# A tile's scale moved from VectorE to TensorE, and the first tile in two parts, at the start of an encoder layer

## The chip, the cores and the metric

The kernel runs on one core of a Trainium2 chip. The metric is the device time of one execution in microseconds (us), as the median of several runs. A profiled execution gives a trace of every instruction of the core's engines: TensorE (PE for matmuls, PEld for the weight loads ahead of them), VectorE (DVE), ScalarE (ACT), GpSimd (POOL), SyncE (SP, which issues DMAs), and of the transfers.

## What is computed

One layer of an encoder on x of 1024 tokens by 1024 channels, all in float32. What matters here is its beginning:

```
mod = silu(c) @ w_ada + b_ada                  # six vectors of 1024: sh1, sc1, gt1, sh2, sc2, gt2
h   = rmsnorm(x, norm1_g) * (1 + sc1) + sh1
z   = h @ w_in                                 # u, v, q, k, va and two gates
```

After that come a gated MLP branch and a windowed attention branch on z, a merge, an output projection, and a SwiGLU feed-forward layer that is modulated in the same way by the other vectors. The output has the shape of x.

## The kernel before, in words

Channels lie on the 128 partitions and tokens along the free axis, so x is eight tiles of 128 channels (k = 0 to 7) by 512 tokens for the first half of the tokens. Products keep float32 accuracy by splitting each operand into a high part (rounded, type fp32r) and a low part (the remainder) and by adding three products: high·high, high·low and low·high.

The part at issue is the first part of `half(0)`, from line 570 on. There `in_order[0]` is true, so each engine issues its instructions in the order of the program text; SP's loads are in program order everywhere. Further on some stretches are in program order and some are ordered by the compiler's scheduler.

Before the tile loop (lines 579 to 654):

- SP issues the loads of x (`xt`, eight tiles), of c (`crow`), of the column constants `cc` (b_ada, two gains, gm_b_s), of r (the rows of w_ada for tile 0's scale and shift, two loads of 512 KB), then, at lines 591 to 595, the first half of `wq0` (256 KB), the scale half of `r1` (rows for tile 1's scale, 512 KB), the first half of `wk0`, the shift half of `r1`, and the second half of `wq0`. More `r` loads and weight units follow inside the loop (`r4`, in the text below, is the first pair that comes as one load of 1024 KB: the rows for tile 4).
- The squares of x are made on ScalarE (`square`) or VectorE (`square_dve`), added in pairs on VectorE, and summed over channels by TensorE (`column_sums`). ScalarE takes the root, VectorE the reciprocal (`rcol`), and four float32 matmuls spread it over the partitions into the PSUM bank `rp`.
- c is spread over the partitions by TensorE, and ScalarE makes `silu_c` from it (128 x 1024, every partition alike).
- A channel's scale or shift is a dot of one row of w_ada (transposed) with silu(c). `ada_dot` (line 211) does 128 of them at once on VectorE: one product of 128 x 1024 elements with an accumulated sum, into a column of `acc_mod`; a small ScalarE activation then adds bias and gain into a column of `mod`.
- Where TensorE would wait, `open_bank` and `keep_going` add products with zeros into banks that are used later: 7 of them (`ZEROS[2]`) at line 652 behind the four matmuls of `rp`.

In the tile loop (line 665 on), for each k: VectorE scales x by `mod` and by the root's reciprocal (`rp` for k = 0, its copy `rb` in SBUF after), ScalarE adds the shift and rounds to the high part `hH`, VectorE makes low parts of weights and runs `ada_dot` for the scale of tile k + 1, makes the low part `hL` of h, and runs `ada_dot` for the shift of tile k + 1. ScalarE casts weights to high parts between these. TensorE runs the passes of q and k products of tile k: high·high first, which needs `hH` and the high weights. At k = 2 it also sums the squares of the halo (128 tokens of the other half), at k = 4 and 7 it does the halo's products.

All helpers' instructions have line L79 in the profile (L131 for loads), so tiles tell them apart. In the profile's names: `mid<-mid,silu_c` is `ada_dot`; `mid<-mid,mod,at` and `mid<-mid,mod,ss` scale x; ScalarE's `h<-mid,mod` is `hH`, VectorE's `h<-mid,mod,h` is `hL`; `at<-identr,zeros` are the zeros, `at<-ident,rcol` the matmuls of `rp`; `mm<-wh,h` and `mm<-wl,h` are q products.

Of the kernel before, what the change touches and what calls it, by code (L numbers as in the profile page):

```python
# [8 lines left out]
F32 = mybir.dt.float32  # L9
F32R = mybir.dt.float32r  # L10
BF16 = mybir.dt.bfloat16
AF = mybir.ActivationFunctionType
ALU = mybir.AluOpType
# [3 lines left out]
P = 128  # L17
D = 1024
S = 1024
KT = D // P  # L20
HALF = 512
# [15 lines left out]
ZEROS = (9, 2, 7)  # L37
# [4 lines left out]
def kernel(  # L42
# [43 lines left out]
    V, A, G, T = (Engine(e) for e in (nc.vector, nc.scalar, nc.gpsimd, nc.tensor))  # L86
# [3 lines left out]
    const = ctx.enter_context(pool("const"))  # L90
# [17 lines left out]
    def at_bank():  # L108
        return psum.tile([P, 512], F32, tag="at", name=nm("at"))
# [7 lines left out]
    def midt(dt, shape):  # L117
        return mid.tile([P, 2048], dt, tag="mid", name=nm("mid")).rearrange(
            "p (a b) -> p a b", a=shape
        )  # L120
# [9 lines left out]
    def load(dst, src):  # L130
        tc.keep_in_program_order(nc.sync.dma_start(dst, src))  # L131
# [47 lines left out]
    epsc = const.tile([P, 1], F32, tag="epsc", name="epsc")  # L179
    V.memset(epsc, EPS)  # L180

    cc = const.tile([P, 72], F32, tag="cc", name="cc")
    bada, g1c, g2c, bsT = cc[:, :48], cc[:, 48:56], cc[:, 56:64], cc[:, 64:72]
    base = const.tile([P, 48], F32, tag="base", name="base")

    def load_cond():
# [9 lines left out]
    def silu_cond(pcs, i0=0):  # L196
        for i, pc in enumerate(pcs, i0):
            A.activation(silu_c[:, i * 512 : (i + 1) * 512], pc, AF.Silu)
# [9 lines left out]
                                   in1=g, op0=ALU.add, op1=ALU.mult)  # L208
        V.tensor_scalar(base[:, GT1:SH2], bada[:, GT1:SH2], 0.5, None, op0=ALU.mult)

    def ada_dot(r, col, cast=None, then=None):

        c1 = slice(col, col + 1)
        V.scalar_tensor_tensor(
            out=r, in0=r, scalar=1.0, in1=silu_c, op0=ALU.mult, op1=ALU.mult,
            accum_out=acc_mod[:, c1],
        )
        if then is not None:
            then()
        if cast is not None:  # L220
            A.copy(*cast)
        factor, added = 1.0, bada
        if GT1 <= col < SH2:
            factor, added = 0.5, base
        for sc, g in ((SC1, g1c), (SC2, g2c)):
            if sc <= col < sc + 8:
                factor, added = g[:, col - sc : col - sc + 1], base
        A.activation(mod[:, c1], acc_mod[:, c1], AF.Identity, bias=added[:, c1], scale=factor)

    def ada_pair(k):  # L230
        r = midt(F32, 2)
# [59 lines left out]
    def keep_going(bank, one, zero, n):  # L291

        for _ in range(n):
            T.matmul(bank, zero, one.unsqueeze(1).to_broadcast([P, 4, P]), start=False, stop=False)
# [272 lines left out]
    def half(hf):  # L567
# [4 lines left out]
        if hf == 0:  # L572
            in_order[0] = True
            xt2 = [midt(F32, 4) for _ in range(2)]
            xt = [xt2[k // 4][:, k % 4, :] for k in range(KT)]
            halo = midt(F32, 16)
            xh, qh = halo[:, :KT, :], halo[:, KT:, :]
            hl4 = midt(F32R, 16)

            for k, n in ((0, 2), (2, 2), (4, 2), (6, 1), (7, 1)):  # L580
                load(xt2[k // 4][:, k % 4 : k % 4 + n, :].rearrange("p a b -> p (a b)"),
                     xA[:, k * HALF : (k + n) * HALF])
                if k == 2:
                    load_cond()
            hd_store = lambda q, f: f(
                hd[0, q * HALF : (q + 1) * HALF, :].rearrange("(a p) t -> p a t", p=P), xt2[q])
            load(cc, cols)
            r = ada_pair(0)
            wq0, wk0 = (wpool.tile([P, UNIT], F32, tag="raw", name=nm("raw")) for _ in range(2))
            r1 = midt(F32, 2)  # L590
            load(wq0[:, :512], w_q[0][:, :512])
            load(r1[:, 0, :], w_ada1[1, :, :D])
            load(wk0[:, :512], w_kv[0][:, :512])
            load(r1[:, 1, :], w_ada1[1, :, D:])
            load(wq0[:, 512:], w_q[0][:, 512:])
            base_bias = bias_base()
            A.activation(sm(QPK, "es"), ones[:, :QPK], AF.Silu)
            build_bias(*base_bias, range(BIAS))

            total = at_bank()  # L600
            open_bank(total, zeros, zeros)
            keep_going(total, zeros, zeros, ZEROS[0])
            cond = silu_rows()
            sqs = [midt(F32, 4) for _ in range(2)]
            sq = [sqs[k // 4][:, k % 4, :] for k in range(KT)]
            add = lambda i, j: V.tensor_tensor(sq[i], sq[i], sq[j], op=ALU.add)
            square = lambda k: A.activation(sq[k], xt[k], AF.Square)

            def square_dve(k):
                V.tensor_tensor(sq[k], xt[k], xt[k], op=ALU.mult)  # L610

            def column_sums(q, last=False):

                for i in range(NT):
                    T.matmul(total[:, i * P : (i + 1) * P], q[:, i * P : (i + 1) * P], ones,
                             start=False, stop=last and i == NT - 1)

            square(0)
            square(1)
            add(0, 1)  # L620
            column_sums(sq[0])
            square(2)
            square_dve(3)
            add(2, 3)
            column_sums(sq[2])
            square_dve(5)
            square(4)
            silu_cond(cond[:1])
            add(4, 5)
            column_sums(sq[4])  # L630
            square(6)
            square(7)
            silu_cond(cond[1:], 1)
            add(6, 7)
            column_sums(sq[6], True)
            root = sm(5, "ms")
            A.activation(root[:, :NT], total.rearrange("p (a b) -> p a b", b=P)[:, :, 0], AF.Sqrt, scale=1.0 / D, bias=epsc)
            wq, wk = ([wpool.tile([P, UNIT], F32R, tag=x, name=nm(x)) for x in ("wh", "wl")]
                      for _ in range(2))
            ada_dot(r[:, 0, :], SC1, then=ada_base)  # L640
            V.reciprocal(rcol[0][:, :NT], root[:, :NT])
            A.copy(wq[0][:, :512], wq0[:, :512])
            ada_dot(r[:, 1, :], SH1)
            rp = at_bank()
            kbk = [at_bank() for _ in range(2)]
            open_bank(kbk[0], identr, zeros)
            keep_going(kbk[0], identr, zeros, ZEROS[1])
            for i in range(NT):
                T.matmul(rp[:, i * P : (i + 1) * P], rcol[0][:, i : i + 1].to_broadcast([P, P]), ident,
                         start=True, stop=True)  # L650
            open_bank(kbk[1], identr, zeros)
            keep_going(kbk[1], identr, zeros, ZEROS[2])
            hH = [hid(), hid()]
            hL = [hid(), hid()]
        else:
            hH, hL = h_next
            in_order[0] = True
# [7 lines left out]
        for k in range(KT):  # L665
            if hf == 0:
                x = xt[k]
                sh = mod[:, SH1 + k : SH1 + k + 1]
                if k < KT - 1:
                    r = ada_pair(k + 1) if k else r1  # L670
                V.scalar_tensor_tensor(
                    out=x, in0=x, scalar=mod[:, SC1 + k : SC1 + k + 1],
                    in1=rb if k else rp, op0=ALU.mult, op1=ALU.mult)
                A.activation(hH[k // 4][:, k % 4, :], x, AF.Identity, bias=sh)
                def low_part(w, w0, cs):
                    V.tensor_tensor(w[1][:, cs], w0[:, cs], w[0][:, cs].bitcast(F32), op=ALU.subtract)

# [13 lines left out]
                if k == 0:  # L691
                    rb = ss_tile()[:, :HALF]
                    A.copy(rb, rp)
                    tot4 = at_bank()
                    kbk.append(at_bank())
                    kps = [kbk[t // 2][:, (t % 2) * 256 : (t % 2 + 1) * 256] for t in range(nkv)]
                elif k == 2:
                    A.activation(qh, xh, AF.Square)
                elif k == 3:
                    A.activation(root[:, NT:], tot4[:, 0:1], AF.Sqrt, scale=1.0 / D, bias=epsc)  # L700
# [31 lines left out]
                    load(xh.rearrange("p a b -> p (a b)"), xA[:, KT * HALF :])  # L732
                cast = (w_next[0], raw) if src is not None else None
                if k < KT - 1:
                    ada_dot(r[:, 0, :], SC1 + k + 1, cast)
                if k == 3:
                    V.reciprocal(rcol[0][:, NT:], root[:, NT:])
                V.scalar_tensor_tensor(out=hL[k // 4][:, k % 4, :], in0=x, scalar=sh,
# [1185 lines left out]
def _layout(inputs):  # L1924
# [10 lines left out]
    def col(v):  # L1935
        return v.reshape(-1, 128).T

    a = {k: np.asarray(v) for k, v in inputs.items()}
    x = a["x"][0]
# [2 lines left out]
    w_b = a["w_b"][0].reshape(2, 4, 64, 1024).transpose(1, 0, 2, 3).reshape(512, 1024)  # L1942
    w_f = a["w_ffn_in"][0]
    ada = a["w_ada"][0].T.reshape(6, 8, 128, 1024)
    out = {
        "xA": np.concatenate([xt[:, t].reshape(8, 128, -1).transpose(1, 0, 2).reshape(128, -1)
                              for t in (slice(0, 512), slice(512, 640))], axis=1),
        "xB": xt[:, 512:],
        "c": a["c"][0],
        "cols": np.concatenate([col(a["b_ada"][0]), col(a["norm1_g"][0]), col(a["norm2_g"][0]),  # L1950
                                a["gm_b_s"][0].T], axis=1),
        "rowv": np.concatenate([a["gm_v_g"][0], a["q_norm_g"][0], a["k_norm_g"][0],
                                a["attn_sink"][0]]),
        "w_ada1": ada[[1, 0]].transpose(1, 2, 0, 3).reshape(8, 128, 2048),
        "w_ada2": ada[2:].reshape(32, 128, 1024),
        "w_u": tm(w_in[:, 0:512], 2),
        "w_v": tm(w_in[:, 512:1024], 2),
# [32 lines left out]
```

## Time and profile before

| | |
|---|---|
| median of 3 runs | 1226.87 us (1226.71 to 1227.76) |
| profiled execution | 1226.14 us, span in the trace 1224.2 us |
| VectorE busy | 898.1 us (73%) |
| ScalarE busy | 578.9 us (47%) |
| granted TensorE clock | 1.00 of full speed |
| DMA in the first 40 us | 15.03 MB at a mean of 376 GB/s |

The times are device times; the span is that of the instructions in the trace, 1.94 us shorter than the execution's time. All positions in the trace are us from the start of the span. Matmuls are pipelined and the ends of their records are modelled, so TensorE's waits are read from its weight loads.

### The profile page before, as it was taken

The numbers are of one execution on the slowest core, as the hardware profiler recorded it, in microseconds if no ns is written. First come the engines' busy times: TensorE is split into PE (matmuls) and PEld (weight loads), VectorE is DVE, ScalarE is ACT, GpSimd is POOL, SyncE is SP. The second block draws the span as 40 slices with busy tenths as digits, with TensorE's granted clock in tenths as the row PEclk, the third lists the DMA queues.
The fourth block names the chain that finished last, engine by engine and source line by source line (L and its number), as shares of the span: only waits on it lengthen the run. The fifth ranks groups of instructions, "written<-read, shape, count | busy, mean of one in ns | idle before, by whom it ended". The sixth has DMA issues, their size and how long they took to land.

```text
span 1224.2 us, 15615 instructions
## 1 busy us (share of the span) xinstructions
PE 1218.0 (99%) x5693; PEld 1015.8 (83%) x5693; DVE 898.1 (73%) x1450; ACT 578.9 (47%) x944; POOL 148.7 (12%) x178
## 2 busy tenths in 40 slices
PE   9999999999999999999999999999999999999998
PEld 7888888888888888888888888888888888888887
DVE  8988877788878766878797766675676766765646
ACT  5667855367855443635453233333333334433341
POOL 0024323114331000001000001010000000010001
PEclk9999999999999999999999999999999999999999
DMA  9721169621076333597413446445555439995542
GB/s 364 283 87 52 35 235 357 233 86 52 36 273 225 120 105 121 195 317 277 149 52 120 172 155 224 167 174 209 189 189 189 168 150 364 393 368 190 189 172 103
DMA packets 75936, 230.77 MB, mean 189 GB/s; under 512 B 8658, under 2 KB 8914, under 8 KB 71124
## 3 DMA queue, kind: packets, MB, share of 16 engines
q1 hardware_dynamic: 61444, 161.62, 37.4%
q0 software_dynamic: 14416, 68.17, 14.9%
q8 instruction: 44, 0.72, 0.2%
q14 instruction: 32, 0.26, 0.1%
HBM read 174.70 MB, written 55.05 MB: 188 GB/s over the span
## 4 chain that ended last, share of the span: by engine, by line
PE 98%; DMA 0%; DVE 0%; ACT 0%; issue 0%; SPq 0%; DVEq 0%; ACTq 0%
PE mm L79 51%; PE at L79 47%; DMA mid<-in_xA_dram 0%; DVE mid L79 0%; ACT mid L79 0%; ACT wh L79 0%; ACT h L79 0%; DVE crow L79 0%; ACT mod L79 0%; DVE zeros L79 0%; DVE ones L79 0%; SPq L131 0%; DVE identr L79 0%; DVEq L79 0%; ACTq L79 0%
## 5 line engine op out<-in xcount | busy, mean ns | idle before, releaser
L79 PE MATMUL mm<-mid,wh 128*128 128x512 f32 x704 | 217.4, 390 | 0.0
L79 ACT CAST wh<-raw 128x1024 fp32r<-128x1024 f32 (+1 forms) x151 | 154.4, 1024 | 118.7 <-PE mm L79 44.3
L79 DVE TENSOR_TENSOR wl<-raw,wh 128x1024 fp32r<-128x1024 f32 (+1 forms) x137 | 161.5, 1183 | 64.4 <-ACT wh L79 63.9
L79 PEld LDWEIGHTS mm<-mid,wh 128*128 128x128 f32 x704 | 131.7, 188 | 27.1
L79 PE MATMUL mm<-mid,wl 128*128 128x512 f32 x352 | 137.0, 389 | 0.0
L79 PE MATMUL mm<-wh,h 128*128 128x512 f32 x384 | 125.0, 397 | 0.2 <-ACT h L79 0.2
L79 PE MATMUL mm<-h,wh 128*128 128x512 f32 x400 | 123.9, 391 | 0.0
L79 PEld LDWEIGHTS mm<-h,wh 128*128 128x128 f32 x400 | 74.6, 188 | 15.3
L79 PE MATMUL at<-h,wh 128*128 128x512 f32 x272 | 84.0, 390 | 0.0
L79 PEld LDWEIGHTS mm<-wh,h 128*128 128x128 f32 x384 | 70.7, 188 | 14.6 <-ACT h L79 1.2
L79 DVE TENSOR_TENSOR wl<-ws,wh 128x1024 fp32r<-128x1024 f32 (+1 forms) x54 | 60.8, 1125 | 24.7 <-ACT wh L79 24.7
L79 PE MATMUL mm<-h,wl 128*128 128x512 f32 x200 | 77.9, 389 | 0.0
L79 PEld LDWEIGHTS mm<-mid,wl 128*128 128x128 f32 x352 | 66.1, 188 | 13.9
L79 ACT CAST wh<-ws 128x1024 fp32r<-128x1024 f32 (+1 forms) x54 | 52.5, 972 | 43.5 <-DVE ws L79 28.0
L79 PE MATMUL mm<-wl,h 128*128 128x512 f32 x192 | 71.2, 391 | 0.0
L79 ACT ACTIVATE t<-t 128x512 f32<-128x512 f32 x53 | 32.8, 630 | 72.8 <-DVE t L79 72.7
L79 PEld LDWEIGHTS at<-h,wh 128*128 128x128 f32 x272 | 50.9, 188 | 10.5
L79 DVE TENSOR_TENSOR ol<-raw,oh 128x1024 fp32r<-128x1024 f32 x30 | 36.6, 1224 | 30.0 <-ACT oh L79 30.0
L79 ACT ACTIVATE xs<-xs 128x512 f32<-128x512 f32 x21 | 13.3, 632 | 93.5 <-DVE xs L79 93.5
L79 PE MATMUL at<-h,wl 128*128 128x512 f32 x136 | 52.9, 389 | 0.0
L79 PE MATMUL at<-wl,wh 128*128 128x512 f32 (+1 forms) x136 | 52.7, 388 | 0.0
L79 PE MATMUL at<-wh 128*128 128x512 f32 (+1 forms) x136 | 52.7, 387 | 0.0
(271 smaller groups left out, 2731.1 us busy)
## 6 DMA issues: line engine op xcount, KB each, us to landing
raw<-in_w_gate_dram SPq DMA_DIRECT2D x28, 512.0 KB, 3.8
tA<-hid POOLq DMA_DIRECT2D x11, 1024.0 KB, 4.5
tB<-hid POOLq DMA_DIRECT2D x11, 1024.0 KB, 5.0
wo<-in_w_out_dram POOLq DMA_DIRECT2D x22, 512.0 KB, 5.8
wS<-wo POOLq DMA_DIRECT2D x11, 1024.0 KB, 5.1
raw<-wS SPq DMA_DIRECT2D x44, 256.0 KB, 3.3
raw<-tB SPq DMA_DIRECT2D x44, 256.0 KB, 4.5
mid<-in_w_ada_dram SPq DMA_DIRECT2D x20, 512.0 KB, 9.1
```

Of the source, the lines that this page charges most:

```text
L79: ins = f(*args, **kw)
```

## The change

The dot for tile 1's scale leaves VectorE. TensorE does it with eight float32 matmuls, into columns 256 to 383 of the bank `tot4`, whose allocation moves up. They stand where the 7 zero matmuls stood. The stationary operands are 128 x 128 blocks of r1's scale half, whose layout in memory is transposed by blocks for this on the host; the moving operand is one column of `silu_col`, repeated 128 times. `silu_col` is silu of c as 8 columns, and c comes as 8 more columns of `cc` (80 instead of 72). ScalarE's activation for tile 1's scale reads the dot from PSUM.

The load of r1's scale half now goes ahead of the first half of wq0. The square of x's tile 7 goes from ScalarE to VectorE. For k = 0, scaling x and making `hH` are each done in two parts of 256 columns, in turns.

```diff
-    cc = const.tile([P, 72], F32, tag="cc", name="cc")
+    cc = const.tile([P, 80], F32, tag="cc", name="cc")
+    ccol = cc[:, 72:80]
...
-    def ada_dot(r, col, cast=None, then=None):
+    def ada_dot(r, col, cast=None, then=None, dot=None):
         c1 = slice(col, col + 1)
-        V.scalar_tensor_tensor(
-            out=r, in0=r, scalar=1.0, in1=silu_c, op0=ALU.mult, op1=ALU.mult,
-            accum_out=acc_mod[:, c1],
-        )
+        if dot is None:
+            dot = acc_mod[:, c1]
+            V.scalar_tensor_tensor(out=r, in0=r, scalar=1.0, in1=silu_c, op0=ALU.mult, op1=ALU.mult,
+                                   accum_out=dot)
...
-        A.activation(mod[:, c1], acc_mod[:, c1], AF.Identity, bias=added[:, c1], scale=factor)
+        A.activation(mod[:, c1], dot, AF.Identity, bias=added[:, c1], scale=factor)
...
+            load(r1[:, 0, :], w_ada1[1, :, :D])
             load(wq0[:, :512], w_q[0][:, :512])
-            load(r1[:, 0, :], w_ada1[1, :, :D])
             load(wk0[:, :512], w_kv[0][:, :512])
...
             square(6)
-            square(7)
+            square_dve(7)
             silu_cond(cond[1:], 1)
+            silu_col = sm(KT, "silu_col")
+            A.activation(silu_col, ccol, AF.Silu)
...
             open_bank(kbk[1], identr, zeros)
-            keep_going(kbk[1], identr, zeros, ZEROS[2])
+            tot4 = at_bank()
+            dot1 = tot4[:, 2 * P : 3 * P]
+            for i in range(KT):
+                T.matmul(dot1, r1[:, 0, i * P : (i + 1) * P], silu_col[:, i : i + 1].to_broadcast([P, P]),
+                         start=i == 0, stop=i == KT - 1)
...
-                V.scalar_tensor_tensor(
-                    out=x, in0=x, scalar=mod[:, SC1 + k : SC1 + k + 1],
-                    in1=rb if k else rp, op0=ALU.mult, op1=ALU.mult)
-                A.activation(hH[k // 4][:, k % 4, :], x, AF.Identity, bias=sh)
+                for cs in (slice(0, HALF),) if k else (slice(0, 256), slice(256, HALF)):
+                    V.scalar_tensor_tensor(
+                        out=x[:, cs], in0=x[:, cs], scalar=mod[:, SC1 + k : SC1 + k + 1],
+                        in1=(rb if k else rp)[:, cs], op0=ALU.mult, op1=ALU.mult)
+                    A.activation(hH[k // 4][:, k % 4, cs], x[:, cs], AF.Identity, bias=sh)
...
-                    tot4 = at_bank()
...
-                    ada_dot(r[:, 0, :], SC1 + k + 1, cast)
+                    ada_dot(r[:, 0, :], SC1 + k + 1, cast, dot=None if k else dot1[:, :1])
...
+    ada1 = ada[[1, 0]].transpose(1, 2, 0, 3).reshape(8, 128, 2048)
+    ada1[1, :, :1024] = ada[1, 1].reshape(128, 8, 128).transpose(2, 1, 0).reshape(128, 1024)
```

More of the change, by code (lines that the diff above doesn't have):

```diff
@@ L1950, in _layout @@
         "cols": np.concatenate([col(a["b_ada"][0]), col(a["norm1_g"][0]), col(a["norm2_g"][0]),
-                                a["gm_b_s"][0].T], axis=1),
+                                a["gm_b_s"][0].T, col(a["c"][0])], axis=1),
         "rowv": np.concatenate([a["gm_v_g"][0], a["q_norm_g"][0], a["k_norm_g"][0],
                                 a["attn_sink"][0]]),
-        "w_ada1": ada[[1, 0]].transpose(1, 2, 0, 3).reshape(8, 128, 2048),
+        "w_ada1": ada1,
         "w_ada2": ada[2:].reshape(32, 128, 1024),
```

## The prediction

> **What bounds the kernel now.** I read the page first, then the waits of TensorE's weight loads in the first 40 us, then the timeline there engine by engine, then the DMA issues one at a time. The page and, below it, the waits (total, number of times, longest):
>
> ```profile
> span 1224.2 us, 15615 instructions
> PE 1218.0 (99%) x5693; PEld 1015.8 (83%) x5693; DVE 898.1 (73%) x1450; ACT 578.9 (47%) x944; POOL 148.7 (12%) x178
> PE 98%; DMA 0%; DVE 0%; ACT 0%; issue 0%; SPq 0%; DVEq 0%; ACTq 0%
> ```
> ```profile
> PEld mm L79 <- ACT h L79: 1.2, 3, 0.5
> PEld at L79 <- DVE rcol L79: 0.3, 1, 0.3
> PEld at L79 <- ACT mid L79: 0.2, 1, 0.2
> ```
>
> TensorE is busy for 1218.0 of 1224.2 us and 98% of the chain that ended last is its own work. The diff touches only what is issued before about 20 us and takes no matmul of the real work away. So it can win only TensorE's waits behind it: at most 1.2 for h and 0.2 for the square of the halo, 1.4 us or 0.11% of the span. The wait for rcol lies ahead of every moved step and stays.
>
> **The start, as it runs now.** In a timeline a row is: start, busy us, engine, line, operation, out<-in, count, and the idle time before it with its releaser. ScalarE, VectorE, then weight loads:
>
> ```profile
> 12.71 0.62 ACT L79 CAST wh<-raw 128x512 fp32r<-128x512 f32 x1
> 13.78 0.29 ACT L79 ACTIVATE mod<-acc_mod,cc 128x1 f32<-128x1 f32 x1 [0.45 <-DVE mid L79]
> 14.81 0.73 ACT L79 ACTIVATE h<-mid,mod 128x512 fp32r<-128x512 f32 x1 [0.73 <-DVE mid L79]
> 15.44 0.60 ACT L79 CAST wh<-raw 128x512 fp32r<-128x512 f32 x1
> 15.95 0.58 ACT L79 COPY ss<-at 128x512 f32<-128x512 f32 x1
> ```
> ```profile
> 13.97 0.75 DVE L79 SCALAR_TENSOR_TENSOR mid<-mid,mod,at 128x512 f32<-128x512 f32 x1 [0.22 <-PE at L79]
> 14.63 0.69 DVE L79 TENSOR_TENSOR wl<-raw,wh 128x512 fp32r<-128x512 f32 x1
> 15.23 1.22 DVE L79 SCALAR_TENSOR_TENSOR mid<-mid,silu_c 128x1024 f32<-128x1024 f32 x1
> 16.38 0.75 DVE L79 SCALAR_TENSOR_TENSOR h<-mid,mod,h 128x512 fp32r<-128x512 f32 x1
> 17.04 1.22 DVE L79 SCALAR_TENSOR_TENSOR mid<-mid,silu_c 128x1024 f32<-128x1024 f32 x1
> 18.19 0.75 DVE L79 SCALAR_TENSOR_TENSOR mid<-mid,mod,ss 128x512 f32<-128x512 f32 x1
> ```
> ```profile
> 12.68 0.97 PEld L79 LDWEIGHTS at<-ident,rcol 128*128 128x128 f32 x8 [0.30 <-DVE rcol L79]
> 13.57 1.69 PEld L79 LDWEIGHTS at<-identr,zeros 128*128 128x128 f32 x8
> 15.59 0.77 PEld L79 LDWEIGHTS mm<-wh,h 128*128 128x128 f32 x4 [0.33 <-ACT h L79]
> 18.56 0.78 PEld L79 LDWEIGHTS mm<-wl,h 128*128 128x128 f32 x4
> 19.81 0.77 PEld L79 LDWEIGHTS mm<-wh,h 128*128 128x128 f32 x4 [0.47 <-ACT h L79]
> ```
>
> TensorE starts tile 0 (k = 0) at 15.59, as h lands. VectorE has no gap from 13.97 on: scale x0, low part of wq, the dot for tile 1's scale (15.23, removed by the change), low part of h0 (16.38), the dot for tile 1's shift (17.04), scale x1 (18.19). h1 follows, and tile 1 starts at 19.81 after 0.47 of waiting. So at k = 1 VectorE's chain ends last, and the dot at 15.23 holds 16.38 − 15.23 = 1.15 us of it.
>
> **Part 1, the zeros become dots.** Out go 7 zero matmuls; eight in a row start (1.69 − 0.19) / 7 = 0.214 us apart (0.19 is one load). In come 8 fp32 matmuls of 128 columns. The four fp32 matmuls on rcol leave 8 records, so eight leave 16, (0.97 − 0.19) / 7 = 0.111 us apart. After the one zero matmul that opens the bank (13.57 + 0.214 = 13.78) the sixteen end so that the next load can go at 13.78 + 16 × 0.111 = 15.56, against 15.59 now: nothing. Their bounds: 0.111 each as here, which I take since it is the same kind of matmul, or 0.214 each at the zeros' pace, which puts tile 0 at 17.2 and tile 1, (18.56 − 15.59) + 0.8 = 3.77 of work later, at 20.97 instead of 19.81: +1.16, 1228.03 on the median below.
>
> **Part 2, the loads change places.** The dot's half of r1 now goes ahead of wq0's first half on SP's one queue; the transfers behind the pair keep their place. Issues and, below, KB and us to landing, in the same order (the r1 half at 6.09 shows no landing):
>
> ```profile
> 4.48 0.59 SPq L131 DMA_DIRECT2D mid<-in_w_ada_dram  x1
> 5.72 0.33 SPq L131 DMA_DIRECT2D raw<-in_w_q_dram  x1
> 6.09 0.48 SPq L131 DMA_DIRECT2D mid<-in_w_ada_dram  x1
> 8.02 0.33 SPq L131 DMA_DIRECT2D raw<-in_w_kv_dram  x1
> 8.66 0.33 SPq L131 DMA_DIRECT2D mid<-in_w_ada_dram  x1
> ```
> ```profile
> mid<-in_w_ada_dram SPq DMA_DIRECT2D x1, 512.0 KB, 7.6
> raw<-in_w_q_dram SPq DMA_DIRECT2D x1, 256.0 KB, 7.0
> raw<-in_w_kv_dram SPq DMA_DIRECT2D x1, 256.0 KB, 6.8
> mid<-in_w_ada_dram SPq DMA_DIRECT2D x1, 512.0 KB, 7.5
> ```
>
> Landings: 4.48 + 7.6 = 12.08, wq0 at 5.72 + 7.0 = 12.72 (0.64 for 256 KB, so about 1.28 for 512), wk0 at 14.82, r1's other half at 16.16. So in the new order I estimate r1's half at 12.08 + 1.28 = 13.36 and wq0 at 14.0, both below wk0's 14.82, which is the upper end for either. The dots need r1 at 13.78: covered by 0.4. But ScalarE casts wq0 at 12.71, the moment it lands, and now casts at 14.0. Queued behind that cast on ScalarE are mod (tile 0's shift) and h0. A cast holds ScalarE 15.95 − 15.44 = 0.51, so mod goes at 14.51 and h0's first half at 14.51 + 0.29 = 14.80 or a little after, at 14.81 now. **The halves of h0 are thus eaten by the load that was pushed back.**
>
> **Part 3, two parts of 256 columns.** No row shows a 256-column part of this activation; bounds are half of 0.73 (0.37) and all of it. I take 0.52, nearer the lower end as the 512-column op is mostly columns; h0's first half ends at about 15.34, the second, overlapping slightly, at 15.82 (from 15.54 down to 16.3 at the ends). TensorE, free at 15.56, needs the second half only two weight loads of 0.2 later: no loss. On VectorE two halves of x0 cost between 0.66 (14.63 − 13.97) and 1.32, beside the wait for wq's cast, which ends only at 14.6, and then for h0: hidden.
>
> **Part 4, VectorE without the dot.** The low part of h0 can go once h0's second half is done, about 15.86 against 16.38: 0.52 earlier, not the 1.15 removed. Then the shift dot starts at 16.52 (its data lands at 16.16), x1 0.52 earlier at 17.67, h1 and tile 1 at 19.29. TensorE's own work for tile 0 is done at 15.56 + 3.77 = 19.33 at the latest. So TensorE reaches tile 1 **0.5 us** earlier. mod for tile 1's scale waits for dots and ScalarE (cast and copy from 15.8 on, 1.1 long), near 17.0: ahead of 17.67.
>
> **What is late next.** The gain must pass tiles 3 to 5. VectorE and ScalarE, weight load, then the r4 issue and its landing:
>
> ```profile
> 28.36 0.76 DVE L79 SCALAR_TENSOR_TENSOR mid<-mid,mod,ss 128x512 f32<-128x512 f32 x1
> 29.02 1.23 DVE L79 SCALAR_TENSOR_TENSOR mid<-mid,silu_c 128x1024 f32<-128x1024 f32 x1
> ```
> ```profile
> 39.11 0.72 ACT L79 ACTIVATE h<-mid,mod 128x512 fp32r<-128x512 f32 x1 [0.69 <-DVE mid L79]
> ```
> ```profile
> 39.89 0.76 PEld L79 LDWEIGHTS mm<-wh,h 128*128 128x128 f32 x4 [0.37 <-ACT h L79]
> ```
> ```profile
> 16.90 0.33 SPq L131 DMA_DIRECT2D mid<-in_w_ada_dram  x1
> ```
> ```profile
> mid<-in_w_ada_dram SPq DMA_DIRECT2D x1, 1024.0 KB, 11.8
> ```
>
> r4 lands at 16.90 + 11.8 = 28.70 and its dot starts at 29.02, straight behind x3. The transfers keep their bytes and the queue is full, so r4 stays at 28.70: VectorE can be at most 29.02 − 28.72 = 0.30 earlier from there. At 39.89 TensorE waits once more for h (0.37), at the end of that same VectorE and ScalarE chain, so only **0.30** of the 0.5 survives tile 5. After that TensorE is busy without such a wait.
>
> **Small edits, costed at nothing.** square(7) on VectorE starts when the sum before it ends; silu_col is an activation of 8 columns under ScalarE's wait for the column sums; cc grows by 8 columns. The rows that cover the first two:
>
> ```profile
> 10.21 0.69 DVE L79 TENSOR_TENSOR mid<-mid 128x512 f32<-128x512 f32 x1 [0.70 <-ACT mid L79]
> 12.15 0.26 ACT L79 ACTIVATE ms<-at,epsc 128x4 f32<-128x4 f32 x1 [0.19 <-PE at L79]
> ```
>
> VectorE's 0.70 idle before 10.21 holds a product of 0.69, so the sum starts at 10.2 as before (a loss of a second such product, 0.69, would pass straight to the end if the cover were gone; x7 landing late is the one way). ScalarE loses a whole square of 512 columns ahead of 12.15 and gains 8 columns, so its wait there only grows.
>
> **Sum.** Parts 1 and 3 nothing, part 4 −0.52, cut to −0.30 at tile 5. Against the profiled execution (span 1224.2, 1226.14 us as timed) 1225.84. That run is 0.73 under the median of the three, 1226.87; on the median the forecast is **1226.57**.
>
> **Rivals.**
> A. *All of VectorE's gain goes through* (r4 is early or tile 5's wait is TensorE's own): −0.52, up to the whole 1.4: 1226.35 to 1225.47. For it: 1.4 us of waits hang on this chain. Against: r4's landing, 0.3 under its use.
> B. *The wait moves to wq0, and the result is slower.* Place: ScalarE's cast of wq0, with mod and h0 behind it. Price: each us of landing beyond 14.0 moves h0's second half and the low part by the same. The gain of 0.52 is gone at 14.0 + 0.52 = 14.52; from there it is slower us for us. By the upper end, 14.82, that is +0.30: 1227.17. For it: it needs no new mechanism, only that the pair shares the engines. Against: landings one after another, 0.64 after 12.08. At 14.3 to 14.5 the change does nothing that it says: 0 to −0.2.
> C. *TensorE's clock drops.* The zeros may be there to keep it up. In the first zeros ten loads took 3.92, 0.414 apart, against 0.214 later:
>
> ```profile
> 1.86 3.92 PEld L79 LDWEIGHTS at<-zeros 128*128 128x128 f32 x10 [1.86 <-DVE identr L79]
> ```
>
> At half pace the 3.77 of tile 0 become 7.54, and tile 1 starts at 15.56 + 7.54 = 23.10 instead of 19.81: at most +3.29, 1230.16. Against: the rcol matmuls are of the dots' kind, and the zeros right behind them run at 0.214. [...] No row of this kernel has dots.
> D. *Other work shifts*: past the tile loop the order is not all by hand, and a wait may appear or go; I take ±0.5, the size of the largest wait quoted (0.47).
>
> **Chances.** Forecast (−0.1 to −0.45) 0.50; A 0.20; B 0.18, half of it near zero; C 0.04; D beyond ±0.5 0.08. 0.2% is 2.45 us, about what a measurement of this kernel can tell from no change. No case but unknown gains of D comes under it; C and the worst of D go over it. Faster 0.03, same 0.91, slower 0.06. The range goes from A's end (1225.47) to B's end with the 0.89 by which the highest of the runs before, 1227.76, is over the median: 1227.17 + 0.89 = 1228.06; C is left out.
>
> **What would show it.** In the changed kernel: wq0's cast near 14.0 instead of 12.71; dots about 0.11 apart from 13.8; first weight load of tile 0 near 15.56; low part of h0 near 15.86; tile 1 near 19.3 with almost no wait; the dot on r4 near 28.7 with VectorE idle before it; tile 5 near 39.6. Wrong if the dots wait for r1 (a gap after 13.78), if wq0 lands past 14.5, if the zeros' pace of 0.214 shows in the dots, or if TensorE's waits after 55 us differ by more than 0.5.

## The result, and the profile after

The changed kernel takes 1233.78 us (median of 6 runs, 1232.7 to 1234.72) against 1226.79 us for the kernel before in the same job (6 runs, 1225.9 to 1227.76): a ratio of 1.0057, with a 95% interval of 1.0047 to 1.0068. It is 7.0 us slower, where the forecast was 1226.57 and the range ended at 1228.06.

The page of the changed kernel, the same lines as were shown of before:

```profile
span 1232.8 us, 15634 instructions
PE 1225.8 (99%) x5702; PEld 1016.3 (82%) x5702; DVE 898.1 (73%) x1450; ACT 578.5 (47%) x945; POOL 148.7 (12%) x178
PE 95%; DMA 3%; issue 1%; DVE 1%; ACT 0%; POOL 0%; SPq 0%; POOLq 0%; DVEq 0%; ACTq 0%
```

The profiled execution's span is 8.6 us longer (it is the slowest of the six runs), and TensorE's busy time is longer by 7.8. TensorE is idle for 7.0 us in all, against 6.2 before, so nearly all of the loss is its own work, which has become longer. Only nine matmul records were added. So I read the span in windows. Columns: window, length, then busy us and instructions of PE, PEld, DVE, ACT and POOL, then granted clock, DMA share and GB/s. First the changed kernel, then before:

```profile
200.00:300.00 100.00, 99.99 (x528) 85.42 (x527) 80.11 (x183) 55.37 (x121) 24.08 (x20) 1.00 0.45 170
700.00:800.00 100.00, 100.00 (x437) 81.72 (x436) 64.31 (x88) 34.40 (x48) 7.46 (x14) 1.00 0.48 173
```
```profile
200.00:300.00 100.00, 99.96 (x528) 85.40 (x527) 79.26 (x182) 55.49 (x122) 23.92 (x19) 1.00 0.45 169
700.00:800.00 100.00, 100.00 (x443) 82.81 (x442) 66.78 (x92) 33.22 (x46) 8.53 (x16) 1.00 0.50 179
```

From 200 to 300 us both kernels start 528 matmuls. From 700 to 800 us, in the feed-forward layer, TensorE is busy all the time in both at a clock of 1.00, and yet 437 matmuls fit where 443 did. **The same matmuls have become slower, far behind the last instruction that the diff touches.** Which ones, the groups by shape say (busy us, mean ns). The changed kernel, then before:

```profile
L79 PE MATMUL mm<-h,wh 128*128 128x512 f32 x400 | 123.9, 391 | 0.0
L79 PE MATMUL at<-tt1h,wh 128*128 128x512 f32 x112 | 44.2, 395 | 0.0
L79 PE MATMUL at<-b22l,wh 128*128 128x512 f32 x112 | 44.1, 394 | 0.0
```
```profile
L79 PE MATMUL mm<-h,wh 128*128 128x512 f32 x400 | 123.9, 391 | 0.0
L79 PE MATMUL at<-tt1h,wh 128*128 128x512 f32 x112 | 43.7, 390 | 0.0
L79 PE MATMUL at<-b22l,wh 128*128 128x512 f32 x112 | 43.6, 389 | 0.0
```

Products of weights with `h` have not moved. Products of weights with the tiles of the feed-forward pool (`tt1`, `tt2`, `b22`, each as a high and a low tile) have 5 ns more. A record's length is modelled for a pipelined matmul (389 to 395 ns in these groups, while a new one starts every 227 to 233); the distance between starts isn't. One stretch of weight loads, each followed by its matmul (start, busy us), in the changed kernel and then before:

```profile
709.63 0.41 PEld L79 LDWEIGHTS at<-h,wh 128*128 128x128 f32 x2
...
715.07 0.19 PEld L79 LDWEIGHTS at<-tt2h,wh 128*128 128x128 f32 x1
...
717.86 0.19 PEld L79 LDWEIGHTS at<-tt1h,wh 128*128 128x128 f32 x1
```
```profile
711.22 0.19 PEld L79 LDWEIGHTS at<-tt2h,wh 128*128 128x128 f32 x1
...
713.94 0.19 PEld L79 LDWEIGHTS at<-tt1h,wh 128*128 128x128 f32 x1
```

From the first load on `tt2h` to the first on `tt1h` there are 12 loads: (717.86 − 715.07) / 12 = 0.2325 us apart now, (713.94 − 711.22) / 12 = 0.2267 before. On `h`, 24 loads ahead in the changed kernel, (715.07 − 709.63) / 24 = 0.2267. Over the whole trace I took the distance from the start of each 512-column matmul to the start of the next, where that has 512 columns too, as a mean by the two tiles that the first of them reads:

| tiles read (records) | before, ns | changed, ns | difference in all, us |
|---|---|---|---|
| weights with feed-forward tiles (1008) | 226.9 | 232.8 | +5.9 |
| feed-forward tiles with `h` (48) | 227.9 | 232.4 | +0.2 |
| weights with `h` or `mid` (2762) | 228.6 | 229.0 | +1.1 |
| weights with weights (556) | 226.7 | 227.0 | +0.2 |

That is 7.4 of the span's 8.6 us. Another 0.67 comes at the start: tile 1 begins at 20.48 instead of 19.81. About 0.5 is not assigned.

What the diff does to all of these: `silu_col` has its own name in the pool of small tiles, which holds four buffers of each name, so this tile of 32 bytes per partition takes 128. `cc` is 32 bytes longer. Tiles allocated behind them move up. The addresses that the compiler gave, in bytes per partition and with the remainder by 256:

| kernel | weights `wh` | `h` | first `mid` | `tt1h` | feed-forward less weights, mod 256 |
|---|---|---|---|---|---|
| before | 31936 (192) | 56512 (192) | 89280 (192) | 191680 (192) | 0 |
| changed | 31968 (224) | 56544 (224) | 89312 (224) | 191840 (96) | 128 |

The pool of small tiles lies between `mid` and the feed-forward pool. Before, the weight tiles, `h`, `mid` and the feed-forward tiles all had the same remainder. In the changed kernel the feed-forward tiles are 128 off from the other three.

The start of the changed kernel, which the prediction was about, answers line by line to the rows shown of before (ScalarE, VectorE, weight loads, in one timeline):

```profile
12.74 0.97 PEld L79 LDWEIGHTS at<-ident,rcol 128*128 128x128 f32 x8 [0.30 <-DVE rcol L79]
...
14.03 0.87 DVE L79 SCALAR_TENSOR_TENSOR mid<-mid,mod,at 128x256 f32<-128x256 f32 x2 [0.22 <-PE at L79]
14.66 1.86 PEld L79 LDWEIGHTS at<-silu_col,mid 128*128 128x128 f32 x16 [0.83 <-issue]
15.26 0.62 ACT L79 CAST wh<-raw 128x512 fp32r<-128x512 f32 x1 [2.50 <-DMA raw<-in_w_q_dram]
16.11 0.91 ACT L79 ACTIVATE h<-mid,mod 128x256 fp32r<-128x256 f32 x2
16.66 0.76 PEld L79 LDWEIGHTS mm<-wh,h 128*128 128x128 f32 x4
...
17.05 0.75 DVE L79 SCALAR_TENSOR_TENSOR h<-mid,mod,h 128x512 fp32r<-128x512 f32 x1 [0.45 <-ACT h L79]
...
20.48 0.53 PEld L79 LDWEIGHTS mm<-wh,h 128*128 128x128 f32 x3 [0.26 <-ACT h L79]
```

Both loads landed late here: wq0's cast goes at 15.26 after 2.50 us of waiting for its DMA, and the dots start at 14.66 (the matmul record names the DMA of r1, 0.55 us of waiting). Tile 0 starts at 16.66 instead of 15.59. 0.4 of that is made up by tile 1.

### The profile page after: what moved, and what is told of

Read it like the earlier page. It is cut to its first block, busy times and chain, and to the rows that moved or that the text cites. A ratio compares the mean times of both kernels' runs of the same rounds, so it can differ in the third digit from the quotient of the medians.

```text
span 1232.8 us, 15634 instructions
## 1 busy us (share of the span) xinstructions
PE 1225.8 (99%) x5702; PEld 1016.3 (82%) x5702; DVE 898.1 (73%) x1450; ACT 578.5 (47%) x945; POOL 148.7 (12%) x178
## 4 chain that ended last, share of the span: by engine, by line
PE 95%; DMA 3%; issue 1%; DVE 1%; ACT 0%; POOL 0%; SPq 0%; POOLq 0%; DVEq 0%; ACTq 0%
PE mm L79 49%; PE at L79 46%; DMA wS<-wo 1%; DMA mid<-in_w_ada_dram 1%; DMA wo<-in_w_out_dram 1%; DMA mid<-in_xA_dram 0%; DVE ws L79 0%; DVE wl L79 0%; DVE mid L79 0%; ACT mid L79 0%; DVE hid L79 0%; DVE wo L79 0%; ACT wh L79 0%; ACT h L79 0%; DVE xs L79 0%
## 5 line engine op out<-in xcount | busy, mean ns | idle before, releaser
L79 PE MATMUL at<-wh,wl 128*128 128x512 f32 (+1 forms) x136 | 52.8, 388 | 0.0
```

Source lines behind the costliest of these rows:

```text
L79: ins = f(*args, **kw)
```

## The experiments

**Theory.** The loss is the distance between the addresses of the two operands of a matmul, weights and feed-forward tiles, and has nothing to do with the dots or the loads. **Rivals.** One: the start's delay, through a load that lands late, sets later work back. Two: the absolute address counts, or the larger `cc`. Three: something in the new matmuls (a column repeated 128 times) or in the order of later work does it. In the expectations the theory is called the offset theory, rivals one and three the start theory, and rival two, as a matter of 64-byte boundaries, the boundary theory. All kernels below compute the whole layer; padding tiles are written once by GpSimd and never read. Each is compared with runs of the kernel before on the same chip.

### The unused tile alone, and the longer constant alone

`pad128` is the kernel before with a tile of the same size and name as `silu_col`, and nothing else of the change. `cc80` is the kernel before with `cc` of 80 columns.

```diff
+            G.memset(sm(KT, "silu_col"), 0.0)
```
```diff
-    cc = const.tile([P, 72], F32, tag="cc", name="cc")
+    cc = const.tile([P, 80], F32, tag="cc", name="cc")[:, :72]
```

> The kernel before with one thing added: an unused tile of 8 columns in the pool of small tiles (four buffers of 32 bytes, one memset on GpSimd). All its tiles up to that pool keep their addresses; those of the attention and feed-forward pools behind it move up by 128 bytes, still on 64-byte boundaries. Offset theory (the loss comes from feed-forward tiles that no longer lie a multiple of 512 bytes from the weight tiles): the matmuls on these tiles start 232 to 233 ns apart instead of 227, some 1056 of them, so about +6.3 us, 1233. Boundary theory (the loss comes from tiles that lie 32 bytes off a 64-byte boundary): no change, 1226.8 within 0.5. Start theory (the loss comes from the dots and loads at the start): no change.

> The kernel before with the constant tile cc 80 columns wide instead of 72, the 8 columns unused. Every large tile moves up by 32 bytes, off the 64-byte boundary, all by the same amount. Offset theory: no change, 1226.8 within 0.5. Boundary theory: 227 becomes 232 to 233 ns on the feed-forward tiles or on all, +6.3 us or more. Start theory: no change.

Measured: `pad128` 1234.34 us (4 runs), ratio 1.0058, 95% 1.0044 to 1.0072. `cc80` 1226.72 us, ratio 1.0000, 0.9991 to 1.0009. Windows of `pad128`, then `cc80`:

```profile
700.00:800.00 100.00, 100.00 (x437) 81.75 (x436) 63.40 (x88) 34.31 (x47) 8.53 (x16) 1.00 0.49 174
```
```profile
700.00:800.00 100.00, 100.00 (x443) 82.84 (x442) 66.81 (x92) 33.33 (x46) 8.53 (x16) 1.00 0.50 179
```

437 matmuls again with a tile that nobody reads, and 443 with all large tiles moved by 32 bytes together. The four distances of `pad128` are those of the changed kernel to a tenth (232.8, 232.4, 229.0, 227.0 ns). Its span, 1231.2, is 7.0 longer than before: 7.4 by the table, less 0.5 by which it reached rcol earlier (12.18 instead of 12.68). **The unused tile reproduces the whole loss, so rivals one and three are not needed for it. `cc80` has all large tiles off a 64-byte boundary and loses nothing, which speaks against rival two;** the last group of runs settles it.

### The change without its shift

`col_const` is the changed kernel with `silu_col` among the constants, which lie ahead of all large tiles. `col_const_noswap` also puts the two loads back in their old order. `after_pad384` keeps `silu_col` where the change has it and adds 384 bytes behind it, so that the feed-forward tiles are 512 off instead of 128.

```diff
+    silu_col = const.tile([P, KT], F32, tag="silu_col", name="silu_col")
...
-            silu_col = sm(KT, "silu_col")
```
```diff
-            load(r1[:, 0, :], w_ada1[1, :, :D])
             load(wq0[:, :512], w_q[0][:, :512])
+            load(r1[:, 0, :], w_ada1[1, :, :D])
```
```diff
             silu_col = sm(KT, "silu_col")
             A.activation(silu_col, ccol, AF.Silu)
+            G.memset(small.tile([P, 96], F32, tag="pad", name="spad", bufs=1), 0.0)
```

> The changed kernel with silu_col in the pool of constants instead of the pool of small tiles, nothing else. All large tiles move together by 64 bytes against the kernel before. Offset theory: the feed-forward matmuls are back at 227 ns; what is left is the start, where the changed kernel reached tile 1 at 20.48 instead of 19.81: 1226.8 + 0.7 or a little less, about 1227.3. Boundary theory: the tiles are on 64-byte boundaries again, so the same 1227.3. Start theory: 1233.8 as the changed kernel.

> As the one before, and the two loads in the order of the kernel before (wq0's first half, then r1's scale half). By the view that wq0's late cast holds h0 at the start: wq0 is cast near 12.7 again, r1 lands near 14.0 and the dots end near 15.8, so tile 0 starts near 15.9 and the low part of h0 near 15.6; tile 1 near 19.4; 0.3 to 0.6 less than with the loads exchanged, about 1226.6. If the order of the two loads does not matter: the same time as the run before within 0.2.

> The changed kernel, silu_col in the small pool as it is, and 384 bytes of padding behind it, so that the feed-forward tiles lie 512 bytes further from the weights than in the kernel before; all large tiles are 32 bytes off a 64-byte boundary. Offset theory with a period of 512 bytes: 227 ns again and 1226.7 as with silu_col among the constants. Without a period: 1233.8 as the changed kernel.

Measured: `col_const` 1226.65 us (11 runs), ratio 0.9998, 0.9989 to 1.0007. `col_const_noswap` 1226.96 us (11 runs), 1.0000, 0.9991 to 1.0008. `after_pad384` 1228.01 us (10 runs), 1.0008, 0.9999 to 1.0018. Windows of `col_const`, then `after_pad384`:

```profile
700.00:800.00 100.00, 100.00 (x443) 82.81 (x442) 66.97 (x92) 33.37 (x46) 8.53 (x16) 1.00 0.50 179
```
```profile
700.00:800.00 100.00, 100.00 (x443) 82.81 (x442) 66.31 (x91) 32.92 (x47) 8.56 (x16) 1.00 0.49 180
```

Both are back at 443 and at 226.9 ns, with the dots, the exchange and the halves all in place. In `after_pad384` the feed-forward tiles are farther from the weights than in the changed kernel, moved by 512 bytes instead of 128, so a greater distance is not a greater loss.

What the change is worth without the shift is read from the start. `col_const`, then `after_pad384`, then `col_const_noswap`:

```profile
13.15 0.97 PEld L79 LDWEIGHTS at<-ident,rcol 128*128 128x128 f32 x8 [0.30 <-DVE rcol L79]
13.40 0.62 ACT L79 CAST wh<-raw 128x512 fp32r<-128x512 f32 x1 [0.24 <-DMA raw<-in_w_q_dram]
...
14.14 1.99 PEld L79 LDWEIGHTS at<-silu_col,mid 128*128 128x128 f32 x16
...
16.06 0.76 PEld L79 LDWEIGHTS mm<-wh,h 128*128 128x128 f32 x4
...
18.61 0.72 ACT L79 ACTIVATE h<-mid,mod 128x512 fp32r<-128x512 f32 x1 [0.43 <-DVE mid L79]
...
19.66 0.88 PEld L79 LDWEIGHTS mm<-wh,h 128*128 128x128 f32 x4
```
```profile
12.50 0.97 PEld L79 LDWEIGHTS at<-ident,rcol 128*128 128x128 f32 x8 [0.30 <-DVE rcol L79]
...
14.93 0.62 ACT L79 CAST wh<-raw 128x512 fp32r<-128x512 f32 x1 [2.41 <-DMA raw<-in_w_q_dram]
...
20.16 0.76 PEld L79 LDWEIGHTS mm<-wh,h 128*128 128x128 f32 x4 [0.24 <-ACT h L79]
```
```profile
12.84 0.97 PEld L79 LDWEIGHTS at<-ident,rcol 128*128 128x128 f32 x8 [0.29 <-DVE rcol L79]
...
15.39 1.86 PEld L79 LDWEIGHTS at<-silu_col,mid 128*128 128x128 f32 x16 [1.48 <-ACT h L79]
...
17.18 0.76 PEld L79 LDWEIGHTS mm<-wh,h 128*128 128x128 f32 x4
```

Executions reach rcol at different times (12.18 to 13.15), so I count from there to tile 1. Before takes 19.81 − 12.68 = 7.13 (`cc80` 7.12, `pad128` 7.12). `col_const` takes 19.66 − 13.15 = 6.51 and does not wait for h at either tile: a gain of 0.62. The changed kernel's own execution took 20.48 − 12.74 = 7.74, a loss of 0.61, and `after_pad384` 20.16 − 12.50 = 7.66, a loss of 0.53, with the same instructions; what differs is wq0's landing, cast at 15.26 and 14.93 there and at 13.40 in `col_const`. So of three executions with this start one gains and two lose. Without the exchange the dots stand 1.48 us (the weight load's row puts it down to h, the matmul's own record to the DMA of r1's half, 1.19 us), and tile 1 begins at 20.78, 7.94 after rcol. The expectation had it the other way, tile 1 near 19.4. None of this shows in the medians, whose intervals are about ±0.1%, 1.1 us.

### The two halves

```diff
-                for cs in (slice(0, HALF),) if k else (slice(0, 256), slice(256, HALF)):
+                for cs in (slice(0, HALF),):
```

> The changed kernel with silu_col among the constants, and tile 0 scaled and shifted in one part of 512 columns as before; read in the first 45 us. If the two parts are hidden behind wq0's cast, as predicted: the low part of h0 and tile 1 lie as far behind the first weight load on rcol as with the two parts (6.5 us to tile 1), within 0.2. If they carry the gain: tile 1 later by 0.3 or more.

One execution, 1226.28 us, span 1224.5. Its first tile:

```profile
14.48 0.62 ACT L79 CAST wh<-raw 128x512 fp32r<-128x512 f32 x1 [1.96 <-DMA raw<-in_w_q_dram]
15.32 0.72 ACT L79 ACTIVATE h<-mid,mod 128x512 fp32r<-128x512 f32 x1
...
16.10 0.76 PEld L79 LDWEIGHTS mm<-wh,h 128*128 128x128 f32 x4 [0.61 <-ACT h L79]
```

Tile 0 waits 0.61 for the whole h; of the kernels with halves, `after_pad384` waits 0.65 there and `col_const` and the changed kernel do not. Tile 1 begins 7.18 after rcol, 0.67 behind `col_const`, which by the expectation would be the halves' gain. But wq0 landed at 14.48 in this execution, against 13.40 in `col_const`. What part of this is the halves' and what the load's cannot be told from one execution: inconclusive.

### One distance for each tile: two stairs

To see several distances in one run, the six feed-forward tiles were given different ones by unused tiles between them: in `stairs` 0 (`b22h`), 32, 64, 96, 128 and 192 bytes, in `stairs2` 256 (`b22h`), 288, 320, 384, 448 and 512.

```diff
-        (t1h, t1l), (t2h, t2l), (b22h, b22l) = ((fpt(f"{n}h"), fpt(f"{n}l")) for n in ("tt1", "tt2", "b22"))
+        t1h = fpt("tt1h")
+        ffn_pad(8)
+        t1l = fpt("tt1l")
...
+        b22h, b22l = fpt("b22h"), fpt("b22l")
```

> The kernel before with unused tiles between the tiles of the feed-forward pool, so that against the weights (counted in the kernel before as 0) they lie at b22h 0, b22l 32, tt1h 64, tt1l 96, tt2h 128, tt2l 192 bytes; one look, read by the start-to-start time of the matmuls that stream each tile. Offset theory: b22h at 227 ns, tt2h at 232 to 233 as in the changed kernel, and the others show from which offset on it is slow. Boundary theory (only tiles off a 64-byte boundary are slow): b22l and tt1l slow, tt1h, tt2h and tt2l at 227. Time by the offset theory between 1227 and 1233.

> The same with larger steps: b22h 256, b22l 288, tt1h 320, tt1l 384, tt2h 448, tt2l 512 bytes. Offset theory with a period of 512 bytes: tt2l back at 227 ns, b22h to tt2h slow in part. If only the distance from 0 counts, without a period: all slow.

One execution each: 1232.44 and 1232.82 us (before 1227.19 in that job). Groups of `stairs`, where `b22h` has not moved at all:

```profile
L79 PE MATMUL at<-tt1h,wh 128*128 128x512 f32 x112 | 44.5, 397 | 0.0
L79 PE MATMUL at<-b22h,wh 128*128 128x512 f32 x112 | 44.1, 394 | 0.0
L79 PE MATMUL at<-tt1h,wl 128*128 128x512 f32 x112 | 43.4, 388 | 0.0
```

A miss: `b22h` at distance 0 was to stay at 227 ns and stood at 231.5 with `wh` and 230.5 with `wl`; `tt2l` at 512 in `stairs2` at 234.6. The high and low tiles of a product alternate (high, low, high), so the load for one product runs while the product before it streams (in the kernel before, the load on `tt2h` runs from 711.22 to 711.41, between the start of the matmul ahead of it at 711.22 and of its own at 711.44), and a misplaced tile seems to slow its neighbour in the sequence too. `tt1h` shows the same thing from the other side: 233.1 ns with `wh` and 226.1 with `wl` at one and the same distance of 64. So a tile's own distance does not set the pace of its own matmuls alone, and these two runs can't give a rule by distance. That needs all tiles moved alike.

### All tiles behind the weights moved alike

```diff
+            G.memset(wpool.tile([P, 32], F32, tag="pad", name="wpad", bufs=1), 0.0)
```

This is the kernel before with 128 unused bytes behind the weight tiles, which moves `h`, `mid` and the feed-forward tiles together; the other three have 8, 16 and 64 columns instead of 32.

> The kernel before with an unused tile of 128 bytes behind the weight tiles in their pool: weights stay, all other large tiles (h, mid, attention, feed-forward) move up by 128 bytes together. Offset theory: every product of a weight tile with an h, mid or feed-forward tile goes from 227 to about 233 ns, products of two tiles of one pool (the last stage's wh with wl) stay: some 2700 records more than in the changed kernel, so about +6 x 3800 ns = +20 us or more, 1247 or above. If the slow matmuls of the changed kernel come from the feed-forward tiles' own addresses and not from their distance to the weights: +6.3, 1233.

> As the kernel with 128 bytes behind the weights, with 32 bytes: all large tiles but the weights are 32 bytes further. Which distances cost time is open. If any distance that is not a multiple of 512 bytes is slow: about 1247, products of weights with other tiles at 232 to 233 ns. If only 128 bytes and near it is slow: between 1227 and 1247.

> The same with 64 bytes. If any distance that is not a multiple of 512 is slow: about 1247. If the distance decides by parts of 128 bytes: between 1227 and 1247.

> The same with 256 bytes. Period of 512 bytes: about 1247. Period of 256 bytes: 1227 and 227 ns. If the weights and the streamed tile are best kept apart, faster than 1227.

`weights128`: 1247.11 us (4 runs), ratio 1.0163, 95% 1.0148 to 1.0179. One execution each for the others: `weights32` 1250.99 us, `weights64` 1241.98, `weights256` 1227.12, beside 1226.02 of before. Windows of `weights32`, `weights64`, `weights128` and `weights256`:

```profile
700.00:800.00 100.00, 100.00 (x430) 80.33 (x429) 65.07 (x89) 32.25 (x45) 7.40 (x14) 1.00 0.45 159
```
```profile
700.00:800.00 100.00, 100.00 (x430) 81.03 (x429) 64.31 (x87) 32.79 (x46) 7.35 (x14) 1.00 0.48 169
```
```profile
700.00:800.00 100.00, 100.00 (x432) 81.04 (x431) 65.18 (x90) 33.65 (x46) 7.47 (x14) 1.00 0.47 168
```
```profile
700.00:800.00 100.00, 100.00 (x443) 82.81 (x442) 66.71 (x92) 33.19 (x46) 8.56 (x16) 1.00 0.51 180
```

The distances between starts, in ns, by the two tiles read and by how far the tiles were moved from the weights:

| moved by, bytes | weights with `h` or `mid` | weights with feed-forward tiles | feed-forward tiles with `h` | weights with weights | span, us |
|---|---|---|---|---|---|
| 0 (before) | 228.6 | 226.9 | 227.9 | 226.7 | 1224.2 |
| 32 | 234.4 | 233.3 | 226.8 | 227.7 | 1248.0 |
| 64 | 232.1 | 231.8 | 227.1 | 227.1 | 1239.9 |
| 128 | 233.6 | 232.6 | 226.9 | 227.0 | 1243.6 |
| 256 | 228.7 | 226.9 | 227.6 | 226.7 | 1224.6 |

With 32, 64 and 128 bytes every pair across the pad slows, by 3.5 to 6.4 ns, and every pair on one side of it stays within 1.1: feed-forward tiles with `h` were slow in the changed kernel, where the shift lay between them, and are not here, where they moved together. For 128 bytes the terms are 2762 × 5.0 + 1008 × 5.7 = 19.6 us, and the span grew by 19.4. With 256 bytes all is as before, as with 512 in `after_pad384`. **Of the distances tried, 0, 256 and 512 are free and 32, 64 and 128 are not.**

`weights32` beside `cc80` settles rival two. By the compiler's addresses everything behind the weight tiles lies at the same place in both (`h` at 56544, `tt1h` at 191712); the weights lie at 31936 in `weights32`, as in the kernel before, and at 31968 in `cc80`. The same feed-forward products start 233.3 ns apart in the one and 226.9 in the other, and the times are 1250.99 us (one execution) and 1226.72. So neither the place of the weights nor that of the other tiles decides, but where the two lie relative to each other.

## Why the prediction was wrong

The step that failed is **"Small edits, costed at nothing"**. It priced `silu_col` as "an activation of 8 columns under ScalarE's wait", which is right (0.21 us, hidden), and did not price the memory that it takes. 128 bytes in the wrong pool cost 7.0 us, more than ten times the largest other term of the sum (0.52).

The sentence that let it through stands in the first part: the diff "touches only what is issued before about 20 us", "so it can win only TensorE's waits behind it". That bounds the gain. It does not bound the loss, because an allocation reaches every later instruction that uses a tile behind it. D, "other work shifts", was the right place for it, but was sized by the largest wait quoted, ±0.5, and looked for an order that changes; here the order stayed and 1056 matmuls each took 5.8 ns more. None of the rivals named a slower matmul other than by the clock, and the clock (C) stayed at 1.00. That the zeros keep it up was the author's guess and is not shown: it is 1.00 from 2 to 6 us of the kernel before too, where the first zeros stood 0.414 apart, and from 12 to 25 us of the changed kernel, with the dots in the place of seven zeros.

The other steps, by their own numbers:

- Part 1 held: 16 records of the dots in 1.86 us, (1.86 − 0.19) / 15 = 0.111 apart.
- Part 2's landings were too early for the profiled execution: r1's half was put at 13.36 and held the dots until 14.66, and wq0 was put at 14.0 and was cast at 15.26. Rival B thereby happened in it, past its point of 14.52 by 0.74, and the loss of 0.61 at tile 1 is near that. In the same order wq0 was cast at 13.40 in `col_const`, 14.48 in `col_const_whole` and 14.93 in `after_pad384`, so three of four came after 14.0. A landing taken from one execution was good to about a microsecond, more than the effect that was built on it.
- Part 3: two parts of h took 0.91 together, against 1.02 as forecast (14.80 to 15.82) and 0.73 for the whole. Near in size; its worth stays open.
- Part 4: tile 1 comes 0.62 earlier in `col_const`, forecast 0.52, and without a wait. That the sizes are so near is in part luck. wq0 was cast 0.25 after the first load on rcol there, where the forecast had 14.0 − 12.68 = 1.32; h1 was ready 18.61 + 0.72 − 13.15 = 6.18 after rcol, against 7.07 before, so VectorE's and ScalarE's chain gained 0.89, and TensorE's own work on tile 0 ended last.
- The cut to 0.30 at tile 5 did not come in `col_const`. These are x3 scaled, the dot on r4, and the first load of tile 5:

```profile
27.93 0.76 DVE L79 SCALAR_TENSOR_TENSOR mid<-mid,mod,ss 128x512 f32<-128x512 f32 x1
28.59 1.23 DVE L79 SCALAR_TENSOR_TENSOR mid<-mid,silu_c 128x1024 f32<-128x1024 f32 x1
```
```profile
39.70 0.76 PEld L79 LDWEIGHTS mm<-wh,h 128*128 128x128 f32 x4 [0.38 <-ACT h L79]
```

The dot starts straight behind x3 and ahead of 28.70, where r4's landing was put, so r4 was not what held it. Tile 5 begins 39.70 − 13.15 = 26.55 after rcol, against 39.89 − 12.68 = 27.21 before: the gain there is 0.66, not 0.30. The wait of 0.38 at tile 5 tells nothing, as it is 0.37 before too. What of a gain at the start reaches the end can't be told with these intervals, so the net of −0.30 is neither shown nor refuted.

So without the shift the forecast of "no change that can be measured" would have held: 1226.65 us for `col_const` against 1226.57. That they are this near says nothing for the −0.30: the kernel before took 1226.80 in the same job, and the interval is ±1.1 us.

## What to carry to other kernels

A new tile is a change of layout: before pricing its instructions, ask which pool it is in, times how many buffers, and which tiles lie behind it, and compare the addresses of weights and streamed tiles before and after. When a kernel bound by TensorE gets slower and no wait has grown, count matmuls in equal windows far from the edit; if fewer fit at the same clock, look at the operands, not at the order. Here the remedy costs nothing: the small tile goes ahead of the large ones (1226.65 us), or is padded to 512 bytes in all (1228.01 us; `weights256`, with 256 unused bytes behind the weights, took 1227.12 in one execution).

## What the runs showed of the hardware

- The mean pace of back-to-back 512-column matmuls, with a weight load under each, went with where the two operands lie relative to each other in a partition. For weights with feed-forward tiles it was 226.9 ns where they were moved apart by 0, 256 or 512 bytes, 233.3, 231.8 and 232.6 where by 32, 64 and 128, and 232.8 in the changed kernel, again 128; for weights with `h` or `mid` 228.6 and 228.7 at 0 and 256, and 234.4, 232.1 and 233.6 at 32, 64 and 128. Moving all of them together (`cc80`, 226.9 ns) does nothing. What makes it so, and whether the load takes something from the stream there, no run here shows; that the stairs slowed neighbours of a misplaced tile (`b22h` at distance 0, 231.5 ns) fits a meeting of the operand being loaded with the one being streamed, which is argued and not shown.
- The landing of a load in the first 16 us differed by up to 1.9 us between executions of kernels that issue the same transfers in the same order (wq0 cast, after a wait for its DMA, at 13.40, 14.48, 14.93 and 15.26).
